# Four-layer SSD / FoX / MLA / S5 block in split fp32r: one 512-column matmul for the high weights, deferred work tied behind projections

## The chip, the cores and the metric

One NeuronCore of one Trainium2 chip. The metric is device time in microseconds of one execution; the median of three runs of the kernel before is 2053.08 us (2052.05 to 2055.1).

## The reference

A sequence of 256 tokens of width 2048 passes through four layers, each followed by a residual sum and a layer norm. All weights and activations are fp32.

```python
for i in range(4):
    out = (ssd_mixer, fox_mixer, mla_mixer, s5_mixer)[i](h, ...)
    h = layer_norm(ALPHA * h + out, ln_g[i], ln_b[i])
```

- SSD: `h @ w_in` gives a gate z (4096 columns), conv inputs x (4096), B and C (1024 each) and dt (64); causal width-4 convolution and silu; chunked state-space scan over 64 heads; gate, group RMS norm, `@ w_out`.
- FoX: q, k, v, z (2048 each) and a forget gate f (16); 16 heads of causal softmax attention with a decay term; gate, `@ w_out`.
- MLA: q and kv latents (512 each), rope part, gate z; up-projections; 16 heads of attention; `@ w_out`.
- S5: u and z (2048 each); a diagonal complex recurrence for 128 groups of 16 channels and 64 states; gelu, a gated linear unit (`y @ w_glu`), gate z, `@ w_out`.

## The kernel before, in words

Every large product keeps fp32 accuracy with fp32r matmuls: a weight piece `raw` comes by DMA (512 KB, function `half`, L89), ScalarE rounds it to a high part `whi` (L100), VectorE takes the rest as a low part `wlo` (L101); activations are kept in the same two parts. A product is then three matmuls, high by high, high by low and low by high (`mm3`, L104 to L109). Loads run up to seven buffers ahead, the two parts four buffers ahead.

There are three forms of projection. `proj_tok` (activations stationary, 512 weight columns moving) makes token-major strips, SSD's z, FoX's v and all output projections. `proj_Tk` makes four transposed blocks at once. `proj_T` (L128) makes one transposed 128 x 256 block: for each of 16 k-blocks the weights (128 x 128) are stationary and the 256 columns of the activation move, three times. It serves SSD's x, B, C and dt, FoX's q, k, z and f, MLA's z, S5's z and S5's glu: 144 full projections of 16 k-blocks, and two narrow ones (dt and f). Its result stays in a PSUM bank, which the next step reads in place (the convolution at L466 to L469, the copies at L695, the tanh gates).

What lies between projections (transposes, attention, the S5 scan) is queued with `defer(n, fn)`: `tick` is called after each half projection and runs what is due. That sets the order in which the code emits instructions; a scheduler then orders each engine's queue by priorities.

Names that the prediction speaks of. In FoX, `head` (L684) makes `ckm` (the mask plus the decay row `ck`, loaded by DMA) on GpSimd (POOL), and advances `s5_params`, a generator that prepares the S5 matrices mostly on POOL: each of its 16 steps ends with the tile `pn`, which goes out to `P_d` (L1109), and TensorE (PE) transposes and multiplies the step's tiles (`wp` L1034, `kp` L1041) one step later. In S5, `u_strip` makes four strips ft = 0 to 3; `scan` is a chain of VectorE (DVE) operations on the tiles `X` (L1171 to L1177), spread over ticks by a budget; `y_half` computes the part inside short blocks (`near`, from the tile `shifts`) and the part from the scanned states (`far`, from a tile `mats` loaded from `P_d`), DVE adds them into `ys` (L1352); `back1` transposes `ys` on PE (`yp`, L1361), and so on to gelu. Sixteen gate projections `z_tile` run meanwhile, and after them the 16 `gps` projections of the glu, which need every strip.

Of the kernel before, what the change touches and what calls it, by code (L numbers as in the profile page):

```python
# [11 lines left out]
F32 = mybir.dt.float32  # L12
# [7 lines left out]
P = 128  # L20
# [10 lines left out]
class Core:  # L31


    def __init__(self, tc, ctx, A):
# [13 lines left out]
        self.queue, self.now, self.seq = [], 0, 0  # L48

# [39 lines left out]
    def half(self, src, i, n=2048, spare=None):  # L89

        nc = self.nc
        if self.loads:
            self.loads.pop(0)()
        r = self.raw([P, n // 2], "raw")
        nc.sync.dma_start(r, src[:, i * (n // 2):(i + 1) * (n // 2)])
        if spare:
            hi, lo = (pool.tile([P, n // 2], F32R, tag=t, bufs=b, name=f"w_{t}") for pool, t, b in spare)
        else:
            hi, lo = (self.wp.tile([P, n // 2], F32R, tag=t, bufs=4, name=t) for t in ("whi", "wlo"))
        nc.scalar.copy(hi, r)  # L100
        nc.vector.tensor_tensor(lo, r, hi, op=ALU.subtract)  # L101
        return hi, lo

    def mm3(self, ps, s, m, first, last):  # L104
# [4 lines left out]
        mm(ps, s[1], m[0], start=False, stop=last)  # L109
# [18 lines left out]
    def proj_T(self, src, hT, ps, m=P, order=range(KB)):  # L128
        for _ in self.proj_T_steps(src, hT, ps, m, order):
            pass  # L130

    def proj_tok(self, srcs, aT, n=512, before=None, tail=None, spare=None):
# [10 lines left out]
        while h < N:  # L143
# [9 lines left out]
            for r, (i, t) in enumerate(runs):  # L153
# [4 lines left out]
                for j in range(2):  # L158
                    for tt in range(2) if t is None else (t,):
                        kb = 2 * (h + i) + j  # L160
                        a = [x[kb][:, tt * P:(tt + 1) * P] for x in aT]
# [8 lines left out]
    def proj_Tk(self, srcs, aT):  # L170
# [4 lines left out]
        for q, src in enumerate(srcs):  # L175
            for i in range(2):
                w = self.half(src, i)
                for j in range(2):
                    kb = 4 * q + 2 * i + j
                    a = [x[kb] for x in aT]  # L180
                    for c in range(4):
# [5 lines left out]
                        mm(o, ws[1], a[0], start=False, stop=end)  # L187
# [61 lines left out]
    def first_hT(self):  # L249
# [3 lines left out]
        def load(q):  # L253
            raw = self.raw([P, 2, T], "xraw")
            nc.sync.dma_start(raw, A["xT"][:, 2 * q:2 * q + 2, :])
            for j in range(2):
                nc.scalar.copy(hT[0][2 * q + j], raw[:, j])
                nc.vector.tensor_tensor(hT[1][2 * q + j], raw[:, j], hT[0][2 * q + j], op=ALU.subtract)

        self.loads = [lambda q=q: load(q) for q in range(8)]  # L260
# [6 lines left out]
    def out_layer(self, li, parts, gb_tiles, spare, out=None):  # L267
# [10 lines left out]
        hT = ([None] * KB, [None] * KB)  # L278
# [38 lines left out]
        def turn(t, k0, nk):  # L317
            c = k0 // 4
            if t == 0 and k0 % 4 == 0:
                for i, n in enumerate("hl"):  # L320
                    x = self.hp.tile([P, 4, T], F32R, tag=f"h{n}{c}", name=f"h{n}{c}")
# [1198 lines left out]
```

## Time and profile before

| | |
|---|---|
| profiled execution | 2055.91 us, span of its instructions 2054.1 us |
| TensorE (PE) busy | 98% of the span, 14409 matmuls recorded |
| VectorE (DVE) busy | 67% |
| ScalarE (ACT) busy | 47% |
| GpSimd (POOL) busy | 20% |
| mean granted TensorE clock | 0.992 |
| HBM read | 366.20 MB, 185 GB/s with the writes |

A matmul's row gives a modelled duration that overlaps the next one's; what a matmul costs in a stream is the distance from its start to the start of the next. "Idle before" is how long the engine stood still ahead of an instruction, and the arrow names what it then waited for.

### The profile page before, as it was taken

Reading aid. Unit: us, or ns where it says so; the run is one execution under the profiler, and the core shown is the slowest. Engines: PE = TensorE matmul, PEld = TensorE weight load, DVE = VectorE, ACT = ScalarE, POOL = GpSimd, SP = SyncE. Lnnn points to the kernel's source line nnn. Section 1 sums busy time; section 2 is a strip of 40 time slices with the busy share of each in tenths; the row PEclk is TensorE's granted clock in tenths of the full one; section 3 lists DMA queues with packets and bytes.
Section 4 is the critical chain, followed back from the end, with each engine's and each line's share of the span. In section 5 each row is a group of like instructions: output and inputs, shape, how many; then the busy total and the mean of one; then the engine's idle time right before and its main releaser. Section 6 shows DMA issues by size and latency. Waiting matters only on the chain.

```text
span 2054.1 us, 36447 instructions
## 1 busy us (share of the span) xinstructions
PE 2004.6 (98%) x14409; PEld 1821.1 (89%) x14409; DVE 1383.0 (67%) x2425; ACT 956.7 (47%) x1458; POOL 401.8 (20%) x482
## 2 busy tenths in 40 slices
PE   8999999999999999999999999999999999899997
PEld 7899999999888877999999889998888799899986
DVE  6787777777644695456665566646556778985656
ACT  5455554555433344344444444545544355454432
POOL 0100111001100018999970000000000000010002
PEclk9999999999999999999999999999999999999999
DMA  8555555555665547566665555664347566685662
GB/s 291 180 185 182 184 179 173 189 180 184 219 201 186 181 145 248 166 201 203 191 208 188 183 184 159 197 183 141 109 140 242 182 184 194 179 240 195 190 190 96
DMA packets 115964, 382.70 MB, mean 186 GB/s; under 512 B 18176, under 2 KB 20688, under 8 KB 114000
## 3 DMA queue, kind: packets, MB, share of 16 engines
q1 hardware_dynamic: 103136, 348.11, 53.4%
q0 software_dynamic: 7808, 26.56, 4.1%
q10 hardware_dynamic: 4848, 5.70, 0.8%
q8 instruction: 113, 1.85, 0.4%
q14 instruction: 59, 0.48, 0.1%
HBM read 366.20 MB, written 14.11 MB: 185 GB/s over the span
## 4 chain that ended last, share of the span: by engine, by line
PE 83%; DVE 9%; DMA 3%; POOL 2%; issue 2%; ACT 1%; SPq 0%; DVEq 0%; POOLq 0%; ACTq 0%
PE pt L108 10%; PE pt L109 10%; PE pt L107 10%; PE cps L109 4%; PE cps L108 4%; PE cps L107 4%; PE zps L107 4%; PE zps L108 4%; PE zps L109 4%; DVE wlo L101 2%; PE pk L185 2%; PE pk L186 2%; PE pk L187 2%; PE fox_q L107 2%; PE fox_q L108 2%
## 5 line engine op out<-in xcount | busy, mean ns | idle before, releaser
L101 DVE TENSOR_TENSOR wlo<-raw,whi 128x1024 fp32r<-128x1024 f32 (+3 forms) x611 | 750.8, 1232 | 444.6 <-ACT whi L100 441.7
L100 ACT CAST whi<-raw 128x1024 fp32r<-128x1024 f32 (+3 forms) x611 | 631.6, 1036 | 776.6 <-PE pt L109 320.4
L107 PE MATMUL pt<-whi,hh 128*128 128x512 f32 (+2 forms) x716 | 278.9, 390 | 8.9 <-ACT whi L100 6.9
L108 PE MATMUL pt<-wlo,hh 128*128 128x512 f32 (+2 forms) x716 | 278.7, 389 | 4.2 <-DVE wlo L101 4.2
L109 PE MATMUL pt<-whi,hl 128*128 128x512 f32 (+2 forms) x716 | 275.6, 385 | 0.6 <-DVE hl L330 0.4
L107 PE MATMUL zps<-hh,whi 128*128 128x256 f32 x768 | 221.0, 288 | 0.0
L107 PE MATMUL cps<-hh,whi 128*128 128x256 f32 x768 | 219.9, 286 | 0.0
L108 PE MATMUL zps<-hl,whi 128*128 128x256 f32 x768 | 217.8, 284 | 0.0
L109 PE MATMUL zps<-hh,wlo 128*128 128x256 f32 x768 | 217.8, 284 | 0.0
L109 PE MATMUL cps<-hh,wlo 128*128 128x256 f32 x768 | 217.4, 283 | 0.0
L108 PE MATMUL cps<-hl,whi 128*128 128x256 f32 x768 | 217.3, 283 | 0.0
L107 PEld LDWEIGHTS pt<-whi,hh 128*128 128x128 f32 x716 | 134.8, 188 | 36.2 <-ACT whi L100 6.9
L108 PEld LDWEIGHTS pt<-wlo,hh 128*128 128x128 f32 x716 | 135.0, 188 | 33.7 <-DVE wlo L101 7.3
L109 PEld LDWEIGHTS pt<-whi,hl 128*128 128x128 f32 x716 | 135.1, 189 | 27.5 <-issue 1.9
L107 PEld LDWEIGHTS zps<-hh,whi 128*128 128x128 f32 x768 | 147.9, 193 | 0.6
L108 PEld LDWEIGHTS zps<-hl,whi 128*128 128x128 f32 x768 | 147.9, 193 | 0.0
L109 PEld LDWEIGHTS zps<-hh,wlo 128*128 128x128 f32 x768 | 147.8, 192 | 0.0
L108 PEld LDWEIGHTS cps<-hl,whi 128*128 128x128 f32 x768 | 147.3, 192 | 0.3
L107 PEld LDWEIGHTS cps<-hh,whi 128*128 128x128 f32 x768 | 147.2, 192 | 0.4
L109 PEld LDWEIGHTS cps<-hh,wlo 128*128 128x128 f32 x768 | 147.2, 192 | 0.1
L107 PE MATMUL pt<-whi,yh 128*128 128x512 f32 x240 | 95.5, 398 | 0.0
L108 PE MATMUL pt<-wlo,yh 128*128 128x512 f32 x240 | 95.4, 397 | 0.0
(505 smaller groups left out, 4269.6 us busy)
## 6 DMA issues: line engine op xcount, KB each, us to landing
raw<-in_ssd_z SPq DMA_DIRECT2D x64, 512.0 KB
raw<-in_ssd_x SPq DMA_DIRECT2D x64, 512.0 KB
raw<-in_ssd_o SPq DMA_DIRECT2D x64, 512.0 KB
raw<-in_fox_v SPq DMA_DIRECT2D x32, 512.0 KB
raw<-in_fox_q SPq DMA_DIRECT2D x32, 512.0 KB
raw<-in_fox_k SPq DMA_DIRECT2D x32, 512.0 KB
raw<-in_fox_z SPq DMA_DIRECT2D x32, 512.0 KB
raw<-in_fox_o SPq DMA_DIRECT2D x32, 512.0 KB
```

The source lines that it names most:

```text
L100: nc.scalar.copy(hi, r)
L101: nc.vector.tensor_tensor(lo, r, hi, op=ALU.subtract)
L107: mm(ps, s[0], m[0], start=first, stop=False)
L108: mm(ps, s[0], m[1], start=False, stop=False)
L109: mm(ps, s[1], m[0], start=False, stop=last)
L185: mm(o, ws[0], a[0], start=kb == 0 and c % 2 == 0, stop=False)
L186: mm(o, ws[0], a[1], start=False, stop=False)
L187: mm(o, ws[1], a[0], start=False, stop=end)
```

## The change

- `proj_T` multiplies the high weights with both parts of the activation in one matmul of 512 columns, and the low weights with the high part in one of 256: two matmuls for three. The activation tiles hold both parts (`[P, 2, 4, T]`), the PSUM bank holds two sums, and DVE adds them (`tensor_reduce`) into an SBUF tile, which later steps read. FoX's ScalarE copies of q and k go.
- Deferred work is traced under `issue_after(self.last)`: what it puts on PE stands behind the last matmul of the projection traced so far. `ckm` on POOL stands behind the last `P_d` store. FoX's attention is deferred by two ticks, not one.
- S5: strips' `u` and `un` share one tile; for the last strip `near` is computed before the scan has ended, its loads are issued one strip earlier, both `far` parts follow together in `finish`; `back1` comes two ticks after `far` for strips 0 to 2.
- The first weight piece and the first two activation blocks are loaded and split in halves.

```diff
     def tick(self):
         self.now += 1
         while self.queue and self.queue[0][0] <= self.now:
-            heapq.heappop(self.queue)[3]()
+            self.behind(heapq.heappop(self.queue)[3])
+
+    def behind(self, fn):
+        if self.last is None:
+            return fn()
+        with self.tc.issue_after(self.last):
+            return fn()
...
     def half(self, src, i, n=2048, spare=None):
+        parts = 2 if len(self.loads) == 9 else 1
...
+        for p, c in enumerate(cols):
+            if p:
+                self.loads.pop(0)()
+            nc.sync.dma_start(r[:, c], src[:, i * (n // 2) + c.start:i * (n // 2) + c.stop])
...
     def proj_T_steps(self, src, hT, ps, m=P, order=range(KB)):
+        mm = self.nc.tensor.matmul
...
-                self.mm3(ps, [x[:, j * m:(j + 1) * m] for x in w], [x[order[kb]] for x in hT], kb == 0, kb == KB - 1)
+                hi, lo = (x[:, j * m:(j + 1) * m] for x in w)
+                mm(ps, hi, hT[2][order[kb]], start=kb == 0, stop=False)
+                self.last = mm(ps[:, 0], lo, hT[0][order[kb]], start=False, stop=kb == KB - 1).ins
...
-    def proj_T(self, src, hT, ps, m=P, order=range(KB)):
+    def proj_T(self, src, hT, out, m=P, order=range(KB)):
+        ps = self.acc("pT")[0:m].rearrange("p (n t) -> p n t", n=2)
         for _ in self.proj_T_steps(src, hT, ps, m, order):
             pass
+        self.nc.vector.tensor_reduce(out, ps.rearrange("p n t -> p t n"), AX.X, ALU.add)
...
     def new_hT(self):
-        tiles = [[self.hp.tile([P, 4, T], F32R, tag=f"h{n}{c}", name=f"h{n}{c}") for c in range(4)] for n in "hl"]
-        return tuple([x[k // 4][:, k % 4] for k in range(KB)] for x in tiles)
+        tiles = [self.hp.tile([P, 2, 4, T], F32R, tag=f"h{c}", name=f"h{c}") for c in range(4)]
+        return tuple([tiles[k // 4][:, i, k % 4] for k in range(KB)] for i in (0, 1, slice(0, 2)))
...
             ckm = tp.tile([P, 2, P], F32, tag="ckm", name="ckm")
-            nc.gpsimd.tensor_tensor(ckm, ck, mask, op=ALU.add)
-            next(steps, None)
+            with C.tc.issue_after(C.pool_last):
+                nc.gpsimd.tensor_tensor(ckm, ck, mask, op=ALU.add)
+            C.behind(lambda: next(steps, None))
...
-                ps = C.acc(nm)
-                C.proj_T(A[nm][h], hT, ps[:, 0:T])
                 s = tp.tile([P, T], F32, tag=nm, name=nm)
-                nc.scalar.copy(s, ps[:, 0:T])
+                C.proj_T(A[nm][h], hT, s)
...
-            C.defer(1, C.attend(logits, lambda: V[h // 4], h % 4, finish, shift=cq[:, h, :]))
+            C.defer(2, C.attend(logits, lambda: V[h // 4], h % 4, finish, shift=cq[:, h, :]))
...
         def outputs():
             k, since, tm, pm = held[0]
-            if PIECE[k // 2] in done and C.now >= since + 3:
-                held.pop()
-                if k < 7:
+            wait = 4 if k == 6 else 3 if k < 6 else 1
+            if C.now >= since + wait and (k > 5 or PIECE[k // 2] in done):
+                held.pop(0)
+                if k < 5:
                     y_load(k + 1)
-                y_half(k // 2, k % 2, pm, tm)
+                elif k == 5:
+                    y_load(6)
+                    y_load(7)
+                y_near(k // 2, k % 2, tm)
+                if k < 6:
+                    y_far(k // 2, k % 2, pm)
+                else:
+                    rest.append(pm)
+                    if held:
+                        held[0] = (7, C.now) + held[0][2:]
+                    else:
+                        C.defer(3, finish)
             if held:
                 C.defer(1, outputs)
+        def finish():
+            if len(done) < 3:
+                return C.defer(1, finish)
+            for h2 in range(2):
+                y_far(3, h2, rest[h2])
...
             if h2:
-                C.defer(1, lambda: back1(ft, ys[ft]))
+                C.defer(2 if ft < 3 else 1, lambda: back1(ft, ys[ft]))
```

How instructions stand on three engines, at the places that the prediction rests on.

PE, in FoX's first head, inside the k projection (`fox_k` before; every `proj_T` sum is named `pT` now). Before:

```order
L107 MATMUL fox_k<-hh_7034,whi 128x256
L108 MATMUL fox_k<-hl_7035,whi 128x256
L109 MATMUL fox_k<-hh_7034,wlo 128x256
L107 MATMUL fox_k<-hh_7034,whi 128x256
L108 MATMUL fox_k<-hl_7035,whi 128x256
L109 MATMUL fox_k<-hh_7034,wlo 128x256
```

Now:

```order
L147 MATMUL pT<-h_6344,whi 128x512
L148 MATMUL pT<-h_6344,wlo 128x256
L147 MATMUL pT<-h_6344,whi 128x512
L148 MATMUL pT<-h_6344,wlo 128x256
L147 MATMUL pT<-h_6344,whi 128x512
```

Two k-blocks were six matmuls and are four; the columns that move per k-block stay 768.

POOL, FoX's S5 parameters, where the first heads' `ckm` stand. Before, in the first step:

```order
L1094 TENSOR_TENSOR t_7724<-pw,bb 128x4x64
L1095 TENSOR_TENSOR t_7725<-pw,bb 128x4x64
L688 TENSOR_TENSOR ckm<-ck,mask 128x256 x2
L1096 TENSOR_TENSOR wn<-t_7724,t_7725 128x256
L1098 TENSOR_TENSOR t_7724<-pw,bb 128x4x64
```

Now, behind the store of the third step:

```order
L1126 TENSOR_TENSOR pn<-t_7410,t_7409 128x320
L1080 DMA bc<-in_s_bc 128x256
L1132 DMA P_d<-pn 128x8x64
L714 TENSOR_TENSOR ckm<-ck,mask 128x256
L1101 TENSOR_TENSOR t_7463<-bc,qr 128x4x16
```

The additions that need `ck` no longer stand ahead of three steps of the generator.

DVE, the end of S5's gate projections, around the last additions into `ys`. Before:

```order
L101 TENSOR_TENSOR wlo<-raw,whi 128x1024
L1352 TENSOR_TENSOR ys<-ys,far_20185 128x4x64
L1352 TENSOR_TENSOR ys<-ys,far_20186 128x4x64
L101 TENSOR_TENSOR wlo<-raw,whi 128x1024
L1301 SCALAR_TENSOR_TENSOR zs_16973<-th,zps 128x256
L1352 TENSOR_TENSOR ys<-ys,far_20272 128x4x64
L1352 TENSOR_TENSOR ys<-ys,far_20273 128x4x64
```

Now:

```order
L120 TENSOR_TENSOR wlo<-raw,whi 128x1024
L292 TENSOR_TENSOR y_18224<-gl,y_18224 128x256 x2
L157 TENSOR_REDUCE zs_15274<-pT 128x256
L120 TENSOR_TENSOR wlo<-raw,whi 128x1024
L1324 SCALAR_TENSOR_TENSOR zs_15274<-th,zs_15274 128x256
L1403 TENSOR_TENSOR ys<-ys,far_18304 128x4x64
L1403 TENSOR_TENSOR ys<-ys,far_18305 128x4x64
L1403 TENSOR_TENSOR ys<-ys,far_18340 128x4x64
L1403 TENSOR_TENSOR ys<-ys,far_18341 128x4x64
```

The last four additions stand together, behind all 16 reduces of the gates.

## Rows read from the trace of the kernel before

**Rows 1.** The page: busy time of two engines (part 1), the chain by engine (part 4).

```profile
PE 2004.6 (98%) x14409; PEld 1821.1 (89%) x14409; DVE 1383.0 (67%) x2425; ACT 956.7 (47%) x1458; POOL 401.8 (20%) x482
PE 83%; DVE 9%; DMA 3%; POOL 2%; issue 2%; ACT 1%; SPq 0%; DVEq 0%; POOLq 0%; ACTq 0%
```

**Rows 2.** Timeline, PE, 1000 to 1003 us (start, duration, ...): first and last of 27.

```profile
999.83 0.28 PE L107 MATMUL fox_k<-hh,whi 128*128 128x256 f32 x1
...
1002.95 0.28 PE L109 MATMUL zps<-hh,wlo 128*128 128x256 f32 x1
```

**Rows 3.** Timeline, PE, 100 to 103 us: first and last of 15.

```profile
99.78 0.39 PE L109 MATMUL pt<-whi,hl 128*128 128x512 f32 x1
...
102.95 0.39 PE L108 MATMUL pt<-wlo,hh 128*128 128x512 f32 x1
```

**Rows 4.** Timeline, PE, 600 to 603 us: first and last of 14.

```profile
599.82 0.40 PE L108 MATMUL pt<-wlo,yh 128*128 128x512 f32 x1
...
602.85 0.40 PE L109 MATMUL pt<-whi,yl 128*128 128x512 f32 x1
```

**Rows 5.** Groups of instructions by form, PE, the first of each projection's three matmuls.

```profile
L107 PE MATMUL zps<-hh,whi 128*128 128x256 f32 x768 | 221.0, 288 | 0.0
L107 PE MATMUL cps<-hh,whi 128*128 128x256 f32 x768 | 219.9, 286 | 0.0
L107 PE MATMUL fox_q<-hh,whi 128*128 128x256 f32 x256 | 76.0, 297 | 0.0
L107 PE MATMUL fox_k<-hh,whi 128*128 128x256 f32 x256 | 73.6, 288 | 0.0
L107 PE MATMUL gps<-yh,whi 128*128 128x256 f32 x256 | 73.1, 285 | 0.2 <-ACT yh L264 0.2
```

**Rows 6.** Groups by form, DVE (xcount | busy us, mean ns | idle before).

```profile
L101 DVE TENSOR_TENSOR wlo<-raw,whi 128x1024 fp32r<-128x1024 f32 x585 | 729.1, 1249 | 428.2 <-ACT whi L100 425.5
L282 DVE SCALAR_TENSOR_TENSOR hres<-hres,pt 128x512 f32<-128x512 f32 x32 | 20.8, 682 | 30.0 <-PE pt L109 30.0
L389 DVE TENSOR_REDUCE mx<-lg 128x1 f32<-128x256 f32 x32 | 13.1, 409 | 0.0
```

**Rows 7.** Windows: us, busy (x) of PE, PEld, DVE, ACT, POOL, granted clock, DMA.

```profile
820.04:830.28 10.24, 6.23 (x38) 5.78 (x38) 0.28 (x1) 0.59 (x1) 9.52 (x18) 0.50 0.39 112
1720.00:1830.00 110.00, 103.92 (x1349) 102.09 (x1348) 106.44 (x242) 51.64 (x84) 10.87 (x18) 0.97 0.66 188
128.00:192.00 64.00, 64.00 (x443) 58.90 (x442) 48.69 (x85) 34.66 (x52) 9.07 (x7) 1.00 0.55 181
```

**Rows 8.** Timeline, PE, 815 to 831 us, [idle before <-releaser].

```profile
819.54 0.55 PE L1034 MATMUL wp<-ident,wn 128*128 128x128 f32 x3 [2.85 <-POOL wn L1101]
822.03 0.42 PE L1041 MATMUL kp<-pn,bd 128*32 128x64 f32 x2 [1.94 <-POOL pn L1096]
824.51 1.28 PE L1041 MATMUL kp<-pn,bd 128*32 128x64 f32 x14 [2.07 <-POOL pn L1103]
```

**Rows 9.** Timeline, POOL, 735 to 850 us: the first two `ckm`, the end of the third step.

```profile
772.73 0.73 POOL L688 TENSOR_TENSOR ckm<-ck,mask 128x256 f32<-128x256 f32 x1 [12.44 <-DMA ck<-cum_d]
775.38 1.60 POOL L688 TENSOR_TENSOR ckm<-ck,mask 128x256 f32<-128x256 f32 x1 [1.91 <-DMA ck<-cum_d]
...
823.60 0.86 POOL L1103 TENSOR_TENSOR pn<-t,t 128x320 f32<-128x320 f32 x1
```

**Rows 10.** Timeline, PE, S5: the two long waits among and after the gates.

```profile
1771.59 1.51 PE L1361 MATMUL yp<-ident,ys 128*128 128x128 f32 x6 [5.41 <-DVE ys L1352]
...
1856.07 1.42 PE L1347 MATMUL far<-X,mats 64*64 64x64 f32 x64 [3.12 <-DMA mats<-P_d]
```

**Rows 11.** Timeline, DVE, 30 to 80 us: last work ahead of the second group's strips.

```profile
75.86 1.22 DVE L101 TENSOR_TENSOR wlo<-raw,whi 128x1024 fp32r<-128x1024 f32 x1
```

**Rows 12.** Timeline, PE, 72 to 77 us.

```profile
75.61 0.49 PE L107 MATMUL pt<-whi,hh 128*128 128x512 f32 x1 [1.64 <-DVE conv L469]
```

**Rows 13.** Timeline, ACT, 0 to 32 us: the fifth weight piece.

```profile
18.27 1.05 ACT L100 CAST whi<-raw 128x1024 fp32r<-128x1024 f32 x1 [2.26 <-DMA raw<-in_ssd_z]
```

More of the change, by code (lines that the diff above doesn't have):

```diff
@@ L48, in __init__ @@
         self.queue, self.now, self.seq = [], 0, 0
+        self.last = None
     def defer(self, n, fn, prio=0):
@@ L108, in mm3 @@
         mm(ps, s[0], m[1], start=False, stop=False)
-        mm(ps, s[1], m[0], start=False, stop=last)
+        self.last = mm(ps, s[1], m[0], start=False, stop=last).ins
     def acc(self, name="acc"):
@@ L179, in proj_Tk @@
                     kb = 4 * q + 2 * i + j
[L180 removed]
+                    a = [x[kb] for x in aT[0:2]]
                     for c in range(4):
@@ L186, in proj_Tk @@
                         mm(o, ws[0], a[1], start=False, stop=False)
-                        mm(o, ws[1], a[0], start=False, stop=end)
+                        self.last = mm(o, ws[1], a[0], start=False, stop=end).ins
                 self.tick()
@@ L251, in first_hT, with load @@
         hT = self.new_hT()
[L253 to L260, printed above, removed]
+        def load(k, n=2):
+            raw = self.raw([P, n, T], "xraw")
+            nc.sync.dma_start(raw, A["xT"][:, k:k + n, :])
+            for j in range(n):
+                nc.scalar.copy(hT[0][k + j], raw[:, j])
+                nc.vector.tensor_tensor(hT[1][k + j], raw[:, j], hT[0][k + j], op=ALU.subtract)
+        self.loads = [lambda k=k: load(k, 1) for k in range(2)] + [lambda k=k: load(k) for k in range(2, KB, 2)]
         return hT
@@ L277, in out_layer @@
         gb, mean, nm, rs = [None] * 8, [None] * 2, [None] * 2, [None] * 2
-        hT = ([None] * KB, [None] * KB)
+        hT = tuple([None] * KB for _ in range(3))
         def resid(t, cb, ps):
@@ L319, in turn @@
             if t == 0 and k0 % 4 == 0:
-                for i, n in enumerate("hl"):
-                    x = self.hp.tile([P, 4, T], F32R, tag=f"h{n}{c}", name=f"h{n}{c}")
-                    hT[i][4 * c:4 * c + 4] = [x[:, k] for k in range(4)]
-                    tiles[i].append(x)
+                x = self.hp.tile([P, 2, 4, T], F32R, tag=f"h{c}", name=f"h{c}")
+                for i, n in enumerate((0, 1, slice(0, 2))):
+                    hT[i][4 * c:4 * c + 4] = [x[:, n, k] for k in range(4)]
+                tiles.append(x)
             pt = self.aux("ptr")
@@ L625, in ssd @@
                            [(tp, t, 1, 1) for t in ("xs0", "xs1", "xdt0", "xdt1", "xdd", "st", "gb0", "gb1")],
-                           [[(C.hp, f"h{n}{c}", 1) for n in "hl"] for c in range(4)], out)
+                           [[(C.hp, f"h{c}", 1)] for c in range(4)], out)
 def fox(C, hT, out):
@@ L673, in fox @@
             v_strip(cb)
-            next(steps)
+            C.behind(lambda: next(steps))
         sc = P ** -0.5
@@ L734, in fox @@
                            [(fp, "gb0", 1, 1), (fp, "V3", 1, 1)] + [(pp, t, 1, b) for t, b in (("st", 2), ("st", 2), ("wt", 2), ("wt", 2), ("pn", 3), ("pn", 3))],
-                           [[(C.hp, f"h{n}{c}", 1) for n in "hl"] for c in range(4)], out)
+                           [[(C.hp, f"h{c}", 1)] for c in range(4)], out)
 TWO_PI = 2.0 * math.pi
@@ L1339, in y_half, with y_far @@
                                start=True, stop=True)
+            y = ys[ft][:, 2 * h2:2 * h2 + 2].rearrange("p g a c -> p (g a) c")
+            nc.scalar.copy(y, near.rearrange("p (g c) -> p g c", g=8))
+        def y_far(ft, h2, pm):
+            x = X[PIECE[ft]][:, :, ft - FIRST[PIECE[ft]]]
+            far = [C.aux("far0"), C.aux("far1")]
             for g in range(2):
@@ L1412, in s5 @@
                            [(p, t, 1, 1) for p, t in ((wp, "sc"), (sp, "XC"), (wp, "ut"), (wp, "ys"), (sp, "XA"), (sp, "a4s"), (sp, "zs0"), (sp, "zs1"))],
-                           [((sp, f"ux{c}", 1), (wp if c == 3 else sp, f"un{c}", 1)) for c in range(4)], out)
+                           [((sp, f"xu{c}", 1),) for c in range(4)], out)
 SCAN_US = 1.9
```

90 lines of the change are left out of this document (45 added, 45 removed).

## The prediction

> **What bounds the kernel now.** I read the page's busy times first, then its chain: PE is busy for 98% of the span, and 83% of the chain is PE's [rows 1]. So nearly all the time is matmuls that follow one another, and the rest is a few places where PE stands still. Two questions are left: what does one matmul cost in the stream, and which standstills does the change touch?
>
> For the first I read PE's timeline and not the durations, which overlap. From the first to the last of 27 matmuls with 256 columns lie 26 distances in 3.12 us, 0.1200 us each [rows 2]; for 512 columns 14 distances in 3.17 us, 0.2264 us [rows 3]. Twice the columns cost 0.1064 us more, so a matmul here costs its columns and about 0.0136 us beside. Where the stationary operand is an output tile of a mixer the 512 columns take 13 distances in 3.03 us, 0.233 us [rows 4].
>
> For the second I listed PE's waits. Those in the change's reach are three in FoX's first heads behind POOL [rows 8], two in S5 [rows 10] and those of the start [rows 12, 13].
>
> **The merged matmul.** Per k-block three matmuls of 256 become one of 512 and one of 256. The columns stay 768; one matmul with its weight load goes. The gain is 3 x 0.1200 - (0.2264 + 0.1200) = 0.0136 us. With the dearer 512 columns of [rows 4] it would be 0.007 us, and that is the lower end; I take 0.0136, since the stationary operands here are weights and the moving ones the layer's input, as in [rows 3], and keep the lower end for the range. No row has a moving operand in two pieces, as the high and low parts now are (4 KB apart in the tile): that is a rival below.
>
> A page's rule stands against the change: the Trainium skill, "TensorE: Matmul & The Clock Gate", section "Wait — 56ns, not 53.3ns?", says that a matmul at full clock costs its columns at 2.4 GHz plus some 2.5 ns, wherever it stands in a stream. By it 1952 merges would give back 4.9 us (an estimate from that page) and not the 26.5 us worked out next. The distances in this trace hold 13 ns each, in both sizes, so here I follow the rows.
>
> The matmuls in question are the rows of 768, 768 and three times 256 [rows 5]: 48 projections in SSD, 48 of z in three layers, 16 each for FoX's q and k and the glu, 144 in all, with 16 k-blocks each. Of these I leave out SSD's first six, where another chain sets the end (below), and S5's 16 z, where DVE does. That leaves 122 x 16 = 1952 merges x 0.0136 = **26.5 us**: SSD 9.1, FoX 10.4, MLA 3.5, glu 3.5.
>
> **The added sums.** Each of the 146 projections (two narrow ones included) now ends with a DVE reduce that reads 512 PSUM elements for each of 128 partitions. No such row exists. A reduce of 256 elements takes 0.409 us, an operation over 512 PSUM elements 0.682, one over 1024 SBUF elements 1.249 [rows 6]. I take 0.68, as nearest in size and source; 0.41 and 1.25 are the ends. That is 99 us of DVE work in all, and FoX loses two copies per head on ACT. In SSD DVE is busy 48.69 of 64 us while PE is never idle [rows 7]; a group of six projections brings it to about 53 of 64, or 56 at the upper end. So PE covers it: cost 0. Were the cover gone, 6 x 0.68 = 4.1 us a group would show. The only stretch without cover is S5's, where DVE works 106.44 of 110 us [rows 7].
>
> **Deferred work tied behind projections.** PE's positions hardly move, because what is due stands behind the same half projection as before; FoX's attention comes one tick later, with the z projection to cover it. I count 0, and 1 us either way.
>
> **ckm in FoX.** Before, two `ckm` stand inside the first steps of POOL's generator. POOL waits 12.44 us for the first `ck`, takes 0.73 us for the sum, waits 1.91 and takes 1.60 for the second [rows 9]: 16.7 us in which the steps stand behind it. They end 0.86 us after 823.60 [rows 9], while PE arrives at about 815 and stands still for 2.85 + 1.94 + 2.07 = 6.86 us [rows 8], all behind POOL's `wn` and `pn`. Now the sums stand behind the third step's store. The third `pn` then ends at 824.5 - 16.7 = 807.8, before PE asks. The waits go: 6.86 us. What follows them runs at half clock, 1.2 GHz: from 820.04 to 830.28 the granted clock is 0.50 and PE is busy 6.23 us [rows 7]; at full clock half of that, 3.1 us, is saved. Together **10.0 us**. The moved sums themselves wait for nothing (by 775.38 both `ck` have landed [rows 9]), and their reader, the first head's logits, stands behind q, k and now z, at about 832. The next generator step is queued behind them on POOL: 0.73 + 1.60 us later than it would be, against 7 us of lead. The move passes one queue more, that of POOL's DMA: the `P_d` store is issued ahead of `ckm`, so it is earlier as well.
>
> **S5.** Up to 16 reduces, 11 us at 0.68, join a DVE that is full. Counted along DVE's order, some 0.6 us more stands ahead of the additions into `ys` of the first strip, 1.1 of the second, 3.1 of the third and 9.9 of the last, since those come behind all 16 sums now. Against that: `back1` comes one tick (half a projection, 2.8 us) later, so the 5.41 us wait for `ys` [rows 10] should shrink by about that; and `near` and `shifts` of the last strip leave the end. The 3.12 us wait for `mats` [rows 10] is a load that has to find a free one of three buffers. The last strip's second load still waits for an earlier `far` to free one, so I let it stand. Gains of about 3 and 16 merges x 16 projections x 0.0136 = 3.5 us meet up to 7.3 us of DVE work (16 x 0.68 less the 3.56 us in which DVE was idle). I count **0**, from 7.3 us slower to 5.41 + 3.12 + 3.5 = 12.0 us faster.
>
> **The start.** The first matmul needs a half-size piece, so PE begins a little earlier; but the fifth weight piece comes no sooner, and ACT already waits 2.26 us for it [rows 13]: 0.5 us of gain. Then the first group's chain over DVE sets when the second strip can begin: PE waits 1.64 us [rows 12], with `wlo` done at 75.86 + 1.22 [rows 11]. What the six merged projections ahead of it gain only lengthens this wait, and six reduces stand ahead of that `wlo`, of which I let 1.5 us show. Together **-1.0 us** (a loss), between +1 and -3.
>
> **Sum.** 26.5 + 10.0 + 0 - 1.0 = 35.5 us. The profiled execution took 2055.9 us, 2.8 over the median of 2053.08; 2055.9 - 35.5 = 2020.4, less 2.8 is 2017.6. **Forecast: 2018 us.**
>
> **The rivals.**
> - *A merge returns less.* The 13 ns may belong to the columns' stream rather than to the instruction. At the lower end of 0.007 the merges give 13.7 us, 2030; at nothing, 2053.1 - 9.0 = 2044. Against it: two sizes in like streams give the same 13 ns [rows 2, 3]. For it: the 0.233 us of [rows 4] show that the distance depends on something beside columns. The skill's rule of the clock-gate page, 4.9 us for the merges, falls between the two, at 2039. Chance 0.13, 2028 to 2044.
> - *S5's waits go as well.* If the last strip's early part and the later `back1` free PE wholly, 12 us more: 2006. For it: both waits [rows 10] are on work that the change moves. Against it: DVE is full there. Chance 0.08.
> - *FoX keeps its waits.* The change would not do there what it says if `wn` and `pn` were late because POOL is slow and not because of `ckm`: no gain of 10.0, so 2028. Against it: POOL stood idle 14 us for `ck` [rows 9]. Chance 0.07.
> - *Slower.* One mechanism: reading the two pieces stalls the moving operand in each of 1952 merged matmuls. The kernel breaks even when a merged matmul takes 0.240 + 9.0/1952 = 0.2446 us; at 0.255 it loses 1952 x 0.015 = 29 us against 9 from elsewhere, so 2073. For it, only that no row shows such a read; against it, the bank that it writes is as in [rows 3]. Chance 0.05.
> - The forecast, between 2010 and 2026: 0.67.
>
> **How the numbers follow.** The range of 2006 to 2034 takes in S5's upper end, FoX's waits and the lower end of a merge, and leaves out the slower case and the rest of the small return. 0.2%, about 4 us, is what a measurement of this kernel can tell from no change. Slower by more has 0.04 (the two-piece read, less its mild cases), within it 0.03, faster 0.93.
>
> **What would show it.** In the changed kernel's timeline of PE, merged matmuls should start the next 0.226 us on and the low ones 0.120; 0.233 to 0.240 would speak for the rival of a small return, more than 0.2446 for the two-piece read. Around 800 to 830 us PE should have no wait for `wn` or `pn`, and a granted clock of 1.00. The new group of reduces should show 146 at 0.5 to 0.8 us, in FoX and SSD without an idle PE behind them. In S5 I look at what PE waits for ahead of the last `far` and `yp`, and at DVE's share in the gates. The forecast is wrong if PE's chain loses share to DVE outside S5, or if a merge returns under 0.01 us.

## The result and the profile after

The changed kernel takes 2040.8 us (median of 4 runs, 2038.1 to 2042.0) against 2054.1 of the kernel before (4 runs): ratio 0.9934, 95% interval 0.9922 to 0.9946. It is faster, by 13.3 us and not by the 35.5 that were forecast; 2040.8 lies above the range of 2006 to 2034. The profiled execution took 2042.04 us, its span 2040.2.

The page's busy times and the chain by engine, which answer to [rows 1]:

```profile
PE 1988.5 (97%) x12073; PEld 1695.5 (83%) x12073; DVE 1472.4 (72%) x2572; ACT 957.6 (47%) x1427; POOL 409.7 (20%) x482
PE 82%; DVE 10%; DMA 3%; POOL 2%; issue 2%; ACT 1%; SPq 0%; DVEq 0%; POOLq 0%; ACTq 0%
```

2336 fewer matmuls are recorded, and PE's busy time falls by only 16.1 us. DVE gains 89.4 us of work, and its share of the chain rises by one point. To see where the 13.9 us of span came from I read six places of PE's timeline that both kernels have: the first matmul into `yd` in SSD's first and eighth group, FoX's first q, the transposes that close FoX and those that open S5, and the first matmul of the glu. Before:

```profile
88.68 3.74 PE L576 MATMUL yd<-xdt,arena 128*128 128x64 f32 x32
...
534.87 3.69 PE L576 MATMUL yd<-xdt,arena 128*128 128x64 f32 x32
...
825.72 0.58 PE L107 MATMUL fox_q<-hh,whi 128*128 128x256 f32 x1
...
1237.21 0.63 PE L326 MATMUL ptr<-ident,hres 128*128 128x128 f32 x4
...
1613.82 1.29 PE L326 MATMUL ptr<-ident,hres 128*128 128x128 f32 x8
...
1857.97 0.56 PE L107 MATMUL gps<-yh,whi 128*128 128x256 f32 x1
```

After:

```profile
90.69 3.68 PE L602 MATMUL yd<-xdt,arena 128*128 128x64 f32 x32
...
531.70 3.69 PE L602 MATMUL yd<-xdt,arena 128*128 128x64 f32 x32
...
821.69 0.80 PE L147 MATMUL pT<-h,whi 128*128 128x512 f32 x1
...
1229.20 0.64 PE L353 MATMUL ptr<-ident,hres 128*128 128x128 f32 x4
...
1599.25 1.29 PE L353 MATMUL ptr<-ident,hres 128*128 128x128 f32 x8
...
1846.96 0.78 PE L147 MATMUL pT<-y,whi 128*128 128x512 f32 x1
```

| stretch | forecast, us | measured, us |
|---|---|---|
| start to SSD's first group | +1.0 | +2.0 |
| SSD's first to eighth group | -9.1 | -5.2 |
| eighth group to FoX's first q | -10.0 | -0.9 |
| FoX's q to its closing transposes | -10.4 | -4.0 |
| MLA, to the transposes that open S5 | -3.5 | -6.6 |
| S5, to the glu | 0 | +3.6 |
| glu to the end | -3.5 | -2.9 |
| sum | -35.5 | -13.9 |

Three stretches (SSD's groups, the way to FoX's first q, and FoX) miss 19 of the 21.6 us. MLA and S5 miss by 3.1 and 3.6 us in opposite directions. In MLA's 6.6 us the 256 merges have 3.4 (run 1). The rest is how the kernel before happened to run: it waits 1.86 us for `wlo`, until 1594 us, where the changed kernel waits 0.57 in the same place, and behind that wait its mean granted clock is 0.83 (1590 to 1600 us), against 1.00 in the changed kernel (1576 to 1586). In run 3, whose MLA has the same code as before, MLA takes 2.8 us less. In S5 PE's waits sum to 11.2 us before and 15.2 after, 4.0 us more, while its 256 merges return at most 3.4; the rest of the 3.6 us I can't place.

The start, too, is in part such a difference. Windows of both kernels, 72 to 86 us, before and after (the number ahead of the last two is the mean granted clock):

```profile
72.00:86.00 14.00, 11.33 (x58) 9.06 (x57) 13.41 (x20) 7.17 (x12) 0.00 (x0) 1.00 0.44 125
```

```profile
72.00:86.00 14.00, 11.02 (x47) 8.69 (x46) 13.19 (x21) 7.25 (x11) 0.00 (x0) 0.88 0.36 116
```

In the changed kernel PE has just waited 2.98 us for `wlo`, until 77.30; before, it waited 1.64 and 1.03 us. Some 1.7 of the 2.0 us are clock, by an estimate (14 us by 0.12). The kernel of run 3, whose code is that of the kernel before in this place, shows 0.88 there as well.

The length of the DVE sums is not among the reasons: they take what was estimated (groups by form, DVE).

```profile
L157 DVE TENSOR_REDUCE u<-pT 128x256 f32<-128x512 f32 x48 | 33.0, 687 | 5.9 <-PE pT L148 5.9
L157 DVE TENSOR_REDUCE zs<-pT 128x256 f32<-128x512 f32 x32 | 22.0, 688 | 8.2 <-PE pT L148 8.2
```

**A merged pair has two paces.** Timeline of PE in one of FoX's k projections, from one merged matmul to the third after it:

```profile
930.06 0.40 PE L147 MATMUL pT<-h,whi 128*128 128x512 f32 x1
930.29 0.28 PE L148 MATMUL pT<-h,wlo 128*128 128x256 f32 x1
930.40 0.40 PE L147 MATMUL pT<-h,whi 128*128 128x512 f32 x1
930.64 0.28 PE L148 MATMUL pT<-h,wlo 128*128 128x256 f32 x1
930.75 0.40 PE L147 MATMUL pT<-h,whi 128*128 128x512 f32 x1
931.00 0.28 PE L148 MATMUL pT<-h,wlo 128*128 128x256 f32 x1
931.12 0.40 PE L147 MATMUL pT<-h,whi 128*128 128x512 f32 x1
```

Three pairs take 1.06 us, 353.3 ns each. The same three pairs in MLA's gates:

```profile
1340.02 0.39 PE L147 MATMUL pT<-h,whi 128*128 128x512 f32 x1
...
1341.06 0.39 PE L147 MATMUL pT<-h,whi 128*128 128x512 f32 x1
```

1.04 us, 346.7 ns each. Three matmuls of 256 took 360 ns [rows 2]. So a merge returns 13.3 ns at the one pace, as forecast, and 6.7 at the other, which is the lower end of the forecast. The mean granted clock is 1.00 in both places (830 to 1140 and 1298 to 1376 us). Counted over the trace, an unbroken stream of pairs keeps one of the two paces until something else runs on PE; in FoX 42 of the 46 streams that can be counted have the slow one. In SSD a group has five such streams, and from the third group to the eighth they run slow, fast, fast, slow, slow each time.

**FoX's wait for POOL stayed.** Timelines of POOL and PE (columns: start, duration, engine, line, operation, idle before and its releaser), and the window of what follows:

```profile
771.18 0.79 POOL L1119 TENSOR_TENSOR wn<-t,t 128x256 f32<-128x256 f32 x1 [11.61 <-DVE work L1045]
...
819.57 0.86 POOL L1126 TENSOR_TENSOR pn<-t,t 128x320 f32<-128x320 f32 x1
```

```profile
817.99 0.30 PE L1064 MATMUL kp<-pn,bd 128*32 128x64 f32 x2 [2.79 <-POOL pn L1119]
820.47 1.28 PE L1064 MATMUL kp<-pn,bd 128*32 128x64 f32 x14 [2.19 <-POOL pn L1126]
```

```profile
817.99:826.00 8.01, 5.82 (x29) 4.91 (x30) 0.28 (x1) 0.00 (x0) 7.50 (x15) 0.57 0.55 161
```

`ckm` is gone from in front of the steps, but POOL's first `wn` now waits 11.61 us for DVE: it takes over a buffer in which DVE still computes `work`. The trace of the kernel before has that work of DVE as well, at the end of the same wait:

```profile
772.57 0.21 DVE L1022 TENSOR_TENSOR work<-work 128x64 f32<-128x64 f32 x1
```

It ends at 772.78, and `ckm` began at 772.73 [rows 9]. The third `pn` ends at 820.4, not at 807.8. PE waits 4.98 us, against 6.86 in [rows 8], and runs at a granted clock of 0.57 behind it.

### The profile page after: what moved, and what is told of

Read it like the earlier page. It is cut to its first block, busy times and chain, and to the rows that moved or that the text cites. A ratio compares the mean times of both kernels' runs of the same rounds, so it can differ in the third digit from the quotient of the medians.

```text
span 2040.2 us, 31823 instructions
## 1 busy us (share of the span) xinstructions
PE 1988.5 (97%) x12073; PEld 1695.5 (83%) x12073; DVE 1472.4 (72%) x2572; ACT 957.6 (47%) x1427; POOL 409.7 (20%) x482
## 4 chain that ended last, share of the span: by engine, by line
PE 82%; DVE 10%; DMA 3%; POOL 2%; issue 2%; ACT 1%; SPq 0%; DVEq 0%; POOLq 0%; ACTq 0%
PE pT L147 24%; PE pT L148 12%; PE pt L127 10%; PE pt L126 10%; PE pt L128 10%; DVE wlo L120 3%; PE pk L212 2%; PE pk L214 2%; PE pk L213 2%; PE yd L602 1%; PE lps L898 1%; PE lps L897 1%; DVE hres L339 1%; DVE hres L340 1%; PE o L444 1%
## 5 line engine op out<-in xcount | busy, mean ns | idle before, releaser
L120 DVE TENSOR_TENSOR wlo<-raw,whi 128x1024 fp32r<-128x1024 f32 (+4 forms) x612 | 751.5, 1230 | 340.4 <-ACT whi L119 336.4
L119 ACT CAST whi<-raw 128x1024 fp32r<-128x1024 f32 (+4 forms) x612 | 632.0, 1036 | 730.9 <-PE pt L128 316.9
L147 PE MATMUL pT<-h,whi 128*128 128x512 f32 (+2 forms) x2080 | 744.8, 401 | 0.0
L148 PE MATMUL pT<-h,wlo 128*128 128x256 f32 (+2 forms) x2080 | 585.4, 281 | 3.0 <-DVE wlo L120 3.0
L147 PEld LDWEIGHTS pT<-h,whi 128*128 128x128 f32 (+2 forms) x2080 | 389.6, 187 | 92.8 <-issue 0.2
L148 PEld LDWEIGHTS pT<-h,wlo 128*128 128x128 f32 (+2 forms) x2080 | 392.2, 189 | 4.8 <-DVE wlo L120 3.8
L126 PE MATMUL pt<-whi,h 128*128 128x512 f32 (+2 forms) x716 | 281.0, 393 | 6.5 <-ACT whi L119 6.1
L127 PE MATMUL pt<-wlo,h 128*128 128x512 f32 (+2 forms) x716 | 279.3, 390 | 5.4 <-DVE wlo L120 5.3
L128 PE MATMUL pt<-whi,h 128*128 128x512 f32 (+2 forms) x716 | 276.6, 386 | 0.3 <-DVE h L357 0.3
L127 PEld LDWEIGHTS pt<-wlo,h 128*128 128x128 f32 x716 | 135.9, 190 | 35.2 <-DVE wlo L120 8.4
L126 PEld LDWEIGHTS pt<-whi,h 128*128 128x128 f32 x716 | 135.5, 190 | 34.5 <-ACT whi L119 6.5
L128 PEld LDWEIGHTS pt<-whi,h 128*128 128x128 f32 x716 | 135.8, 190 | 26.9 <-issue 1.7
```

What stands on the lines that cost most here:

```text
L119: nc.scalar.copy(hi[:, c], r[:, c])
L120: nc.vector.tensor_tensor(lo[:, c], r[:, c], hi[:, c], op=ALU.subtract)
L126: mm(ps, s[0], m[0], start=first, stop=False)
L127: mm(ps, s[0], m[1], start=False, stop=False)
L128: self.last = mm(ps, s[1], m[0], start=False, stop=last).ins
L147: mm(ps, hi, hT[2][order[kb]], start=kb == 0, stop=False)
```

## The experiments

Each set of runs was timed beside the kernel before on one chip (medians 2051.9 to 2054.8 in the four sets; the brackets give the ratio to it and its 95% interval). The runs of one kernel spread by 2 to 11 us, so differences below some 4 us are read from stretches of the traces and not from medians.

**1. The merge alone undone.**

```diff
-                mm(ps, hi, hT[2][order[kb]], start=kb == 0, stop=False)
+                mm(ps[:, 0], hi, hT[0][order[kb]], start=kb == 0, stop=False)
+                mm(ps[:, 1], hi, hT[1][order[kb]], start=False, stop=False)
```

> The changed kernel with the merge alone undone: three matmuls of 256 columns per k-block, high by high and low by high into the first sum of the bank, high by low into the second; the DVE sums, the tiles and the order stay. Prediction's price: 13.6 ns for each of 1952 merges on the path, 26.5 us slower than the changed kernel. Theory of two paces: the changed kernel's merged pairs run at 346.7 ns in some stretches and at 353.3 in others, so that the trace's own mean (SSD 350, FoX 353.5, MLA and glu 346.7 against 360) gives 18 to 22 us. Every pair of this kernel's first two matmuls plus the third should be 360 ns in all stretches.

2062.45 us, ratio to before 1.0042 (1.0027 to 1.0057): 21.65 us over the changed kernel. The change has 2336 merges, 32 of them in the two narrow projections: 9.3 ns each by the medians. Of the traces' difference 3.3 us lie ahead of SSD's first `yd`, where kernels with the same code differ as much (run 13); behind it 18.0 us are left for 2224 merges, 8.1 ns each, between the two paces. MLA takes 373.40 us, 3.4 more than in the changed kernel (13 ns a merge), and FoX from q to its closing transposes 411.49 us, to the hundredth what it took before. Without its merges the change would be a loss.

**2. The merge and its sums alone.** `behind` calls its function at once, `ckm` is not tied, attention after one tick, S5's outputs and `back1` as before, first loads whole.

```diff
-        if self.last is None:
-            return fn()
-        with self.tc.issue_after(self.last):
-            return fn()
+        return fn()
...
-        parts = 2 if len(self.loads) == 9 else 1
+        parts = 1
...
```

> The merge and its DVE sums alone, with the work before's order: no tying behind projections, ckm where it stood, FoX's attention one tick later, S5's last strip and back1 as before, first loads whole. Theory: the merge gives some 18 us, FoX's waits behind POOL are back at 6 to 7 us, the start is no later than 1 us, S5 loses what its reordering saved: 2038 to 2044 us. Rival, that the sums are dear where DVE is full and the reordering of S5 is what hides them: 2046 to 2052.

2033.97 us, 0.9905 (0.989 to 0.992), below the 2038 to 2044 that were expected: all the other parts together cost the change 6.8 us by the medians, 6.0 by the two ratios. FoX's stretch takes 404.88 us, 2.6 less than in the changed kernel. `ckm` stands where it stood before, and still PE waits only 5.11 us for `pn` (2.92 and 2.19), against 4.98 in the changed kernel.

**3. `ckm` alone moved, in the kernel before.**

```diff
-            nc.gpsimd.tensor_tensor(ckm, ck, mask, op=ALU.add)
+            with C.tc.issue_after(C.pool_last):
+                nc.gpsimd.tensor_tensor(ckm, ck, mask, op=ALU.add)
...
```

> The kernel before with one edit: ckm on POOL stands behind the last P_d store. Prediction's step: 10.0 us faster, FoX's three waits gone. Theory: the wait for ck hid a second one, POOL's first wn needs a buffer that DVE's work chain still uses until about 771 us, so the third pn comes only some 4 us earlier: 2 to 6 us faster, with two waits of PE left.

2051.77 us, 0.9994 (0.9984 to 1.0003): no change that can be told, neither the 10.0 us of the prediction nor the 2 to 6 of the theory. Timelines of POOL and of PE:

```profile
775.39 0.79 POOL L1097 TENSOR_TENSOR wn<-t,t 128x256 f32<-128x256 f32 x1 [12.64 <-DVE work L1023]
```

```profile
822.31 0.42 PE L1042 MATMUL kp<-pn,bd 128*32 128x64 f32 x2 [2.79 <-POOL pn L1097]
824.80 1.28 PE L1042 MATMUL kp<-pn,bd 128*32 128x64 f32 x14 [2.07 <-POOL pn L1104]
```

POOL waited 12.44 us for `ck` in [rows 9]; with `ck` out of the way it waits 12.64 us for `work`, in the same place. One of PE's three waits goes. From the start of that `wn` to the end of the third `pn` POOL takes 49.4 us, against 47.5 before (776.95 to 824.46), so it loses again part of what it won.

**4 to 6. DVE's chain earlier.** In the changed kernel, two steps a tick; then the steps traced ahead of the first v strip, in the kernel of run 2 with `ckm` tied; then the same with all deferred work tied and S5's new order (so the changed kernel with the attention after one tick and the first loads whole).

```diff
-            C.defer(n, lambda: next(steps))
+            C.defer(n // 2, lambda: next(steps))
```

```diff
+        C.load_small()
+        steps = s5_params(C, pp, pq)
+        for n in range(8):
+            C.defer(n + 3, lambda: next(steps))
         v_strip(0)
...
-        C.load_small()
-        steps = s5_params(C, pp, pq)
-        for n in range(8):
-            C.defer(n, lambda: next(steps))
...
```

> The changed kernel with the first eight steps of the S5 parameter generator due two per tick instead of one, so that DVE's work chain ends earlier. Theory (DVE's chain holds POOL's first wn, and through it PE): POOL's wait of 11.6 us shrinks, the third pn is earlier by the same, PE's waits of 2.79 and 2.19 us at 815 to 820 us go and the half clock behind them: 5 to 8 us faster than the changed kernel. Rival (POOL's own 17.5 us per step sets it): no change within 2 us.

> The merge and its sums alone, with ckm behind the third store and the S5 parameters' first eight steps traced ahead of the first v strip, 10 half projections earlier. Theory (DVE's work chain holds POOL's first wn): POOL has its steps done before PE asks, PE's waits of 2.9 and 2.2 us and the half clock behind them are gone: 2025 to 2028 against 2034 for the merge alone. Rival: the steps delay DVE's layer norm ahead of FoX and PE waits there instead: 2034 or more.

> The changed kernel with the attention due after one tick, the first loads whole, and the S5 parameters' first eight steps traced ahead of the first v strip; TensorE's wp and kp stay tied where they are in the changed kernel (in the run without tying they moved up and PE waited 3.9 and 7.9 us for wn at 750 us). Theory: DVE's chain ends some 10 us earlier, POOL's third pn too, PE's waits of 2.8 and 2.2 us and the half clock go (7 to 8 us), FoX's pace gives 3: 2028 to 2031. Rival: DVE's extra work ahead of FoX makes PE wait for wlo there and eats it: 2034 or more.

2037.63 us (0.992, 0.9903 to 0.9937), 2041.07 (0.9952, 0.9936 to 0.9969) and 2033.15 (0.9889, 0.9874 to 0.9904). In all three PE no longer waits for `wn` or `pn` between 800 and 830 us, so the chain of DVE is what held it. But the wait comes up elsewhere. PE's timeline in the second:

```profile
754.37 0.33 PE L1054 MATMUL wp<-ident,wn 128*128 128x128 f32 x1 [3.71 <-POOL wn L1116]
762.36 0.90 PE L1054 MATMUL wp<-ident,wn 128*128 128x128 f32 x3 [7.66 <-POOL wn L1121]
```

and in the third:

```profile
758.46 0.79 PE L127 MATMUL pt<-wlo,h 128*128 128x512 f32 x1 [5.28 <-DVE wlo L120]
```

In the first PE waits 3.64 us for `wlo`, until 756 us. Untied (the second), PE's `wp` moved up and waited for POOL 11.4 us there. Tied, the earlier steps stand ahead of `wlo` on DVE, and PE waits 5.28 us for that. From the eighth group to FoX's first q the first takes 289.48 us, the second 296.86, the third 291.54, the changed kernel 289.99 and the kernel before 290.85: nothing is won. The expected gains of 5 to 8 us there were wrong; what makes the third fast is FoX's pace (402.57 us for its stretch) and its start.

**7, 8. The attention's second tick,** added to the kernel of run 2, and taken from the changed kernel (the diff is run 8's; run 7's is the other way round).

```diff
-            C.defer(2, C.attend(logits, lambda: V[h // 4], h % 4, finish, shift=cq[:, h, :]))
+            C.defer(1, C.attend(logits, lambda: V[h // 4], h % 4, finish, shift=cq[:, h, :]))
```

> The merge and its sums alone with FoX's attention deferred by two ticks. In the merge alone 12 of 14 q projections behind the kp matmuls run at 346.7 ns a pair, in the changed kernel none. Theory (the logits then stand right ahead of wp and kp, and the stream resumes at the slow pace): FoX's heads 2 to 3 us longer, 2036 to 2037. Rival: tying does it, 2034 here.

> The changed kernel with FoX's attention due one tick after its head again, nothing else. Theory (the second tick puts the logits right ahead of wp and kp, and the q projection then resumes at 353.3 ns a pair): q behind kp and z behind the transposes are mostly at 346.7, FoX's heads 3 us shorter, 2037 to 2038. Rival (tying makes the pace): FoX's heads within 0.5 us of the changed kernel's.

2038.86 us (0.9926, 0.9911 to 0.9941) and 2034.7 (0.9896, 0.988 to 0.9913). FoX's stretch takes 407.09 us with the second tick and 404.28 without it, against 404.88 and 407.52 in the kernels that they come from: 2.2 and 3.2 us, both ways. Behind the `kp` matmuls 13 of 14 q projections run at 346.7 ns a pair without the tick (run 8; 12 in run 2) and none with it. Behind the attention's last matmuls (`o`) 12 of 15 streams are fast without it (runs 2 and 8), and 1 and 2 with it (run 7 and the changed kernel).

**9. Tying alone,** added to run 2 on TensorE.

```diff
-        return fn()
+        if self.last is None:
+            return fn()
+        with self.tc.issue_after(self.last):
+            return fn()
```

> The merge and its sums alone with deferred work tied behind projections added on TensorE, nothing else. Theory A (halved loads): within 1 us of 2034.0. Theory B (tying): 2038 to 2040, with the first group of SSD some 4 us later. If FoX's 3 us (0.2 us per head in the traces) come from tying and not from the attention's second tick, another 3 us: 2041 to 2043 under B, 2037 under A.

2034.52 us (0.991, 0.9887 to 0.9933), FoX's stretch 402.72, 2.2 less than in run 2: tying costs nothing that these runs can tell.

**10. The two parts side by side.**

```diff
-        tiles = [self.hp.tile([P, 2, 4, T], F32R, tag=f"h{c}", name=f"h{c}") for c in range(4)]
+        tiles = [self.hp.tile([P, 4, 2, T], F32R, tag=f"h{c}", name=f"h{c}") for c in range(4)]
...
```

> The changed kernel with the high and low part of a block side by side in the activation tiles (one piece of 512 columns, not two of 256 that lie 4 KB apart), so that the merged matmul reads as the token strips' 512 columns do. Rival of the prediction (the read in two pieces is dear): FoX's pairs fall from 353.3 to 346.7 ns, 768 x 6.7 ns = 5 us, 2035 to 2036. Theory (the pace is set by what the stream resumes behind): FoX's heads stay at 353.3, no change within 3 us.

2040.04 us (0.9941, 0.9925 to 0.9957), FoX's stretch 407.67. Its timeline, three pairs of a FoX projection:

```profile
932.00 0.39 PE L147 MATMUL pT<-h,whi 128*128 128x512 f32 x1
...
933.06 0.40 PE L147 MATMUL pT<-h,whi 128*128 128x512 f32 x1
```

1.06 us as in the changed kernel. The read in two pieces costs nothing.

**11. Interruptions in MLA's gates.**

```diff
+            if h < 15:
+                stop = C.aux("stop")
+                with C.tc.issue_after(C.last):
+                    for t in range(3):
+                        nc.tensor.transpose(stop[:, t * P:(t + 1) * P], C.ident, C.ident)
```

> The changed kernel with three transposes of the identity (128 columns each) tied behind each of MLA's gate projections but the last, whose results nothing reads. Theory (each interruption sets the pace anew): the 15 stretches between them, all at 346.7 ns a pair in the changed kernel, show some or all at 353.3, and none between. Rival (operands, tiles or the load of other engines set it): all stay at 346.7. The transposes themselves cost 15 x some 0.4 us.

2048.21 us in its one run. Two neighbouring projections, with the interruption ahead of each and three pairs:

```profile
1320.92 0.49 PE L875 MATMUL stop<-ident 128*128 128x128 f32 x3
...
1321.60 0.40 PE L147 MATMUL pT<-h,whi 128*128 128x512 f32 x1
...
1322.64 0.39 PE L147 MATMUL pT<-h,whi 128*128 128x512 f32 x1
...
1326.81 0.49 PE L875 MATMUL stop<-ident 128*128 128x128 f32 x3
...
1327.48 0.39 PE L147 MATMUL pT<-h,whi 128*128 128x512 f32 x1
...
1328.54 0.40 PE L147 MATMUL pT<-h,whi 128*128 128x512 f32 x1
```

1.04 us and 1.06 us, with the same activation tiles and the same instructions. Of 14 unbroken projections behind a transpose 8 have the fast pace and 6 the slow one, and none changes within. So the pace is set when the stream resumes. What decides it isn't settled, but it doesn't look like chance: the 14 run slow, slow, slow, and then fast, fast, slow in turn to the end.

**12 to 14. S5 and the start:** S5's gates with three matmuls and no sum, in the changed kernel; S5's new order alone added to run 2; the outputs' old order in the kernel of run 6.

```diff
-            C.proj_T(A["s5_z"][kb], hT, zs[kb])
+            zps = C.acc("zps").rearrange("p (n t) -> p n t", n=2)
+            for _ in C.proj_T_steps(A["s5_z"][kb], hT, zps, three=True):
+                pass
...
```

```diff
-            if PIECE[k // 2] in done and C.now >= since + 3:
+            wait = 4 if k == 6 else 3 if k < 6 else 1
+            if C.now >= since + wait and (k > 5 or PIECE[k // 2] in done):
...
-                C.defer(1, lambda: back1(ft, ys[ft]))
+                C.defer(2 if ft < 3 else 1, lambda: back1(ft, ys[ft]))
```

The second of these diffs is run 13's, and run 14's the other way round.

> The changed kernel with S5's 16 gate projections as before: three matmuls, read from PSUM in place, no DVE sum; all else as changed. Prediction: DVE is full there, so 11 us of sums against 16 x 16 merges cancel: within 3 us. Rival, that the sums set PE's waits in S5 (2.8, 3.0, 3.0 and 3.7 us there): 4 to 8 us faster.

> The merge and its sums alone with the new order of S5's outputs. Prediction: S5's order and sums come out even. From the traces S5 of the changed kernel is 1.0 us behind that of the merge alone, so 2035; if the order was worth what it moves (waits of 5.7, 2.5 and 2.5 us in the merge alone), 2025 to 2029.

> The same with S5's outputs in the order of the kernel before. Prediction's step, S5's order is worth nothing either way: within 2 us of the run before this one. In the profiled runs so far S5 with the new order took 1.5 us less in one pair and 0.8 us more in another.

2046.89 us (0.997, 0.9958 to 0.9981), 2038.88 (0.9929, 0.9914 to 0.9944) and 2034.63 (0.9899, 0.9883 to 0.9916). From the transposes that open S5 to the glu the first takes 251.16 us, the changed kernel 247.71: giving up S5's sums with its merges loses 3.4 us (6.1 by the medians, where less than 3 was expected; 2.5 of it stand at SSD's first `yd` already), which is what 256 merges return at the fast pace. The kernel of run 1, with the sums and without the merges, takes 250.42 us, no more than this one without either, so the sums cost nothing there that can be seen over a scatter of 3 us. Over seven profiles with the new order and six with the old (merged gates in all) this stretch takes 244.7 to 247.7 and 244.85 to 248.0 us, 246.5 on average. In the kernel before it takes 244.15, in that of run 3 245.55. So on these averages S5 lost some 1.6 us though its merges give 3.4 back. PE's waits have grown in run 12 too, to 16.1 us; what lengthened them isn't settled. The second's median is 4.9 us over run 2's, but its trace is 4.2 us behind at SSD's first group already, whose code is the same in both: that is the start's scatter, not S5, in the one execution of four that was traced. Run 14 is 1.5 us over run 6, within the 2 that were expected.

**15. The halved first loads,** added to run 2.

```diff
-        parts = 1
+        parts = 2 if len(self.loads) == 9 else 1
...
-        self.loads = [lambda k=k: load(k) for k in range(0, KB, 2)]
+        self.loads = [lambda k=k: load(k, 1) for k in range(2)] + [lambda k=k: load(k) for k in range(2, KB, 2)]
```

> The merge and its sums alone (2034.0 us before this) with the first loads in halves added. In its trace the changed kernel's first rounding of weights is 1.0 us later than that of the merge alone, and by the second group of SSD it is 5.4 us behind. Theory A, the halved loads cost this: 2039 to 2040. Theory B, tying deferred work behind the projections costs it, in the first group, where DVE and the transposes are the chain: 2034 to 2035 here.

2040.33 us (0.9936, 0.9917 to 0.9955), and at SSD's first `yd` 5.8 us behind run 2. ACT's timeline in the changed kernel, and in run 2 with whole loads:

```profile
4.64 0.61 ACT L119 CAST whi<-raw 128x512 fp32r<-128x512 f32 x1
6.08 0.62 ACT L119 CAST whi<-raw 128x512 fp32r<-128x512 f32 x1 [0.83 <-DMA raw<-in_ssd_z]
...
9.15 1.04 ACT L119 CAST whi<-raw 128x1024 fp32r<-128x1024 f32 x1 [0.52 <-DMA raw<-in_ssd_z]
```

```profile
5.05 1.04 ACT L116 CAST whi<-raw 128x1024 fp32r<-128x1024 f32 x1 [0.55 <-DMA raw<-in_ssd_z]
...
7.88 1.05 ACT L116 CAST whi<-raw 128x1024 fp32r<-128x1024 f32 x1 [1.17 <-DMA raw<-in_ssd_z]
```

The first half is 0.4 us early, the next piece 1.3 us late. How far this carries to the first group is blurred by a DMA: the load of `acs_d`, a scratch tensor from which SSD's tile `arena` is filled and which DVE waits for there. DVE's waits between 36 and 120 us, of the change and of run 2:

```profile
DVE arena L538 <- DMA arena<-acs_d: 6.9, 2, 3.9
```

```profile
DVE arena L535 <- DMA arena<-acs_d: 4.2, 2, 3.0
```

Over seven profiles each (three matmuls per k-block left out), SSD's first `yd` starts at 86.0 to 93.2 us with halves (mean 90.7) and at 85.2 to 91.0 with whole loads (mean 87.8). That load took 6.4 to 9.8 us from issue to landing in ten of the traces. And the granted clock has a part in it: from 72 to 86 us its mean is below 1.00 in six of the seven with halves and in two of the seven with whole loads. Among those eight `yd` starts at 91.5 us on average with halves and at 90.7 without; in the others it starts at 86.0 with halves and at 85.2 to 88.3 without. So the halves cost between nothing and 3 us, and whether they make the clock fall more often, these runs don't show.

## Why the prediction was wrong

**The merge: right in kind, mis-sized.** The term of 26.5 us took 13.6 ns for every merge. 13.3 ns is what the pace of nearly all pairs in MLA's gates and the glu returns; FoX returned 5.2 (4.0 us over 768), SSD from its second to its eighth group 0.77 us a group and so 8.0 ns, and all together 8.1 to 9.3 in run 1, under the 10 that the prediction had named as its sign of being wrong. The step that failed is the choice of 0.0136 over the lower end "since the stationary operands here are weights": merged pairs with the same operands run at either pace (run 11). The y strips [rows 4] are 6.7 ns over [rows 3] for each 512 columns, the same step; whether that comes from their operand isn't shown, since SSD's output strips run at 233.3 ns in every trace. The rival of a small return was the right one in FoX. By the Trainium skill's rule ("TensorE: Matmul & The Clock Gate", "Wait — 56ns, not 53.3ns?") a merge would give 2.5 ns, an estimate from that page: neither pace agrees with it.

**FoX's waits: the step failed.** "The third `pn` then ends at 824.5 - 16.7 = 807.8" took the wait for `ck` as the only one. A wait row names what came last; DVE's `work` ended 0.05 us after `ck` let POOL go, and run 3 shows it in the same place with 12.64 us for 12.44. The term of 10.0 us was worth 1.4 in that run (289.48 us from the eighth group to FoX's q, 290.85 before) and 0.9 in the changed kernel. The rival "FoX keeps its waits" came true, but not by a slow POOL: with DVE's chain earlier the waits at 800 to 830 us go (runs 4 to 6). PE also came to the first wait at 816.7 (819.54 less 2.85 [rows 8]), not at about 815, which changes nothing.

**FoX's attention:** "I count 0, and 1 us either way" failed too. The second tick puts the logits right ahead of `wp` and `kp`, and q, like most of what follows `o`, resumes at the slow pace: 2 to 3 us, both ways (runs 7, 8).

**The start:** a loss of 1.0 became one of 2.0 at the first group, of which some 1.7 are the granted clock, and the second group, counted with 1.3 us of gain, took 0.57 us off, since DVE waits for `acs_d` there too (3.9 us, 3.1 before). No run shows the half us of gain for the halved loads: the next piece came 1.3 us later.

**The sums: right; S5: by luck in the total.** 0.69 us a sum, hidden in SSD, FoX and S5. S5's new order is worth nothing that these runs can tell, but S5 as a whole took 3.6 us longer in the profiled pair, where 0 was counted, and some 1.6 on average; MLA's 3.1 us beyond its term hid that in the total. The waits became others: 2.7 us for `hres` at its opening (1.4 before), 2.8 for `ys`, 3.0 for `wlo`, 3.0 for `yt`, 3.7 for `mats`. The two-piece read and the slower rival fell with run 10.

**Probably not the change's doing:** behind the same 2.80 us wait ahead of FoX the granted clock was 0.81 (715 to 724 us) where it was 1.00 before (718 to 727), which took 1.2 us from that stretch.

The best versions of these, the merge with its sums alone (2034.0), the change with the attention's tick taken back (2034.7) and run 6 (2033.2), lie within 1.6 us of each other and 6 to 8 us ahead of the change.

## What to carry to other kernels

A wait's row shows the releaser that came last: before its length is booked as a gain, look up when every other input and the buffer's last user were done, for the difference to the second is all that can be won. Price an instruction in a stream by start-to-start distances in several stretches, and let a spread between them (here 226 and 233 ns) into the forecast until a run has shown what it depends on: the new code paid the dearer price in most of FoX. And time the parts of a change apart, stretch by stretch: here one part won some 20 us and the others gave 6 to 7 back, and two misses of over 3 us each (MLA and S5) nearly cancelled in the sum.

## What the hardware showed unexpectedly

A stream of merged pairs runs at 346.7 or at 353.3 ns a pair, at full granted clock, for as long as it isn't interrupted; 512-column streams run at 226.7 or 233.3, SSD's output strips at the latter in every trace. The pace changes at interruptions as short as three transposes (0.5 us). It repeats from group to group in SSD and in a regular order in run 11, and yet the same projections take different paces in executions of kernels that don't differ there: in 14 traces the last 192 of the glu's 256 pairs took 66.56 us (four traces) or 67.84 us (ten), 1.3 us apart.
